# Reordering casts and weight loads at the first Strassen pair of each feed-forward block

## The chip, the cores and the metric

One core of a Trainium2 chip runs the whole kernel in one launch. The metric is the device time of that launch in microseconds, the median of several executions. The engines that matter here are TensorE (PE in the profile, with its weight loads as PEld), VectorE (DVE), ScalarE (ACT), GpSimd (POOL) and SyncE (SP); SP and POOL do nothing here but issue transfers from memory. Each engine takes its own instructions strictly in the order in which they were written out, and waits on semaphores for the others.

## The reference, cut to what matters

The computation is a two-layer decoder trunk over 512 tokens of width 1024 in float32. Each layer is a SwiGLU feed-forward block of width 2816, a mixing block (window attention, RWKV-7, short convolution), and a second feed-forward block. The change touches the feed-forward blocks alone:

```python
def swiglu(x, w_in, w_out):
    gate, up = jnp.split(x @ w_in, 2, axis=-1)
    return (jax.nn.silu(gate) * up) @ w_out

h = h + 0.5 * (1.0 + gt1) * swiglu(hn, w_ffn1_in[l], w_ffn1_out[l])
...
h = h + 0.5 * (1.0 + gt3) * swiglu(hn, w_ffn2_in[l], w_ffn2_out[l])
```

There are four such blocks: layer 0 first and second, layer 1 first and second. In the traces the first reads its weights from in_w1i, in_w1p, in_w1o and the second from in_w2i, in_w2p, in_w2o; layer 0 comes before layer 1 in time.

## The kernel before

**Precision.** Every float32 matrix is split into a high and a low part in fp32r. For weights, ScalarE casts the raw tile to `wH` (L104) and VectorE subtracts to get `wL` (L105); `hl` (L393) does both. A product then is three matmuls: high by high, high by low, low by high (L451, L452, L453 in the pairs). So each block of weights (128 x 1024, 512 KB) costs one transfer, one cast and one subtraction before its products can run, and TensorE meets first `wH` (L451) and, two matmuls later, `wL` (L453).

**A feed-forward block.** The 22 column tiles of the gate and up weights are worked off in two groups (`GROUPS`, L36): tiles 0 to 11, then 12 to 21. After each group come its products with the output weights (L93 to L95), whose results go into the residual `h` (L312). In the first group of the first block of layer 0, tiles 0 to 7 are plain products and the pairs begin at pair 4 (`n_first` is 4); in the other three blocks tiles 0 to 3 are plain and the pairs begin at pair 2 (`n_first` is 2). The second group consists of pairs 6 to 10 everywhere.

**A pair.** `pair_in(p)` (L460) computes two gate tiles and two up tiles together by Strassen's scheme with seven products instead of eight. Of the four weight blocks A(0,0), A(0,1), A(1,0), A(1,1) it makes:

- the first sum S = A(1,0) + A(1,1): SP loads the first, POOL adds the second with an accumulating transfer (`plus`, L404); product into `ps_f`, copied out by ScalarE as `up` (L470);
- the first block a11 = A(0,0), in the tile "first"; product into `ps_d`, copied out as `s1` (L474);
- the corner a12 = A(0,1), in a tile "wraw"; product into `ps_g`;
- the second sum S + a11 (VectorE, L475), product into `ps_d` on top of what is there, copied out as `s2` (L489);
- the third block A(0,0) + A(1,0), in the tile "third", again by a load and an accumulating transfer; product into `ps_d`;
- the last sum S + a12 (L502), product into `ps_f`;
- the rest, A(1,1) in a "wraw" tile, whose product (`rest`, L517) is put off and issued inside the next pair by `flush` (L386).

The tile for S alternates between "sum0" and "sum1" from pair to pair. There is one buffer each for "first", "third", "sum0" and "sum1", two for "wraw", and four for `wH` and `wL`. Between the pairs of two groups the tiles "first", "third" and "sum1" are also used for the modulation weights (`wada`, loaded by POOL, read by VectorE at L168).

**What sets the order.** A scheduler writes out the order on each engine from the dependencies and the order of the code; `tc.issue_after(x)` makes the instructions of a block that run on x's engine stand behind x. Before the change, in the first pair of a block with `n_first` 2 (`alone` is then true, L477), the cast of the second sum (`second`, L485) is held behind the copy `s1` (L474); the loads inside pairs are held behind one earlier load of the block in the first two pairs of the first group only (`after`, L565), and are otherwise free.

Of the kernel before, what the change touches and what calls it, by code (L numbers as in the profile page):

```python
# [60 lines left out]
def trunk_kernel(ctx, tc, ins, out, layers=L, phases=("ffn1", "mix", "ffn2")):  # L61
    nc = tc.nc
# [210 lines left out]
    @contextmanager  # L273
    def behind_all(marks):
        with ExitStack() as stack:
            for m in marks:
                stack.enter_context(tc.issue_after(m.ins))
            yield
# [93 lines left out]
    def ffn(l, w_in, w_pair, w_out, hn, im, ss, need, then, ready, first=None, late=None):  # L372
# [6 lines left out]
        with tc.tile_pool(name="act", bufs=1) as ap_:  # L379
# [13 lines left out]
            def hl(w):  # L393
                pair = tuple(wp.tile([P, KD, P], F32R, name=x, tag=x, bufs=4) for x in ("wH", "wL"))
                low[0] = split(*pair, w)
                return pair

            def raw(src, tag=None):
                w = (ap_.tile if tag else wp.tile)([P, KD, P], F32, name=tag or "wraw", tag=tag or "wraw", bufs=1 if tag else 2)
                with tc.issue_after(after[0].ins) if after[0] else nullcontext():  # L400
                    nc.sync.dma_start(w, src)
                return w

            def plus(w, src):  # L404
# [41 lines left out]
            def prod(pt, w, x, start, parts=(0, 1)):  # L446

                for i in parts:
                    for k in range(4):
                        wH, wL = (t[:, 4 * i + k] for t in w)  # L450
                        mm(pt[:, i], wH, x[k][0], start=start and i + k == 0, stop=False, skip_group_check=True)  # L451
                        mm(pt[:, i], wH, x[k][1], start=False, stop=False, skip_group_check=True)  # L452
                        last = mm(pt[:, i], wL, x[k][0], start=False, stop=k == 3, skip_group_check=True)  # L453
                return last
# [5 lines left out]
            def pair_in(p):  # L460
                A = lambda g, kh: w_pair[l, p, g, kh]
                turns = ("r0", "r1") if p % 2 else ("r1", "r0")
                pD, pF, pG = (psum([P, 2, H2], n, t) for n, t in zip(("ps_d", "ps_f", "ps_g"), ("mm",) + turns))
                X = new_x(p)
                half_ = lambda n: E(n).rearrange("p (i t) -> p i t", i=2)
                S = raw(A(1, 0), ("sum0", "sum1")[p % 2])
                plus(S, A(1, 1))
                prod(pF, hl(S), P1, True)
                up = half_("up")
                nc.scalar.copy(up, pF)  # L470
                a11 = raw(A(0, 0), "first")
                prod(pD, hl(a11), B11, True)
                s1 = half_("s1")
                copied = nc.scalar.copy(s1, pD)  # L474
                tt(S, S, a11, ALU.add)  # L475

                alone = p == n_first == 2  # L477
                behind = lambda m: tc.issue_after(m.ins) if p == n_first == 4 else nullcontext()
                if alone:
                    a12 = raw(A(0, 1))  # L480
                    right = hl(a12)
                    front = prod(pG, right, B21, True, (0,))
                flush()
                with tc.issue_after(copied.ins) if alone else nullcontext():
                    second = hl(S)  # L485
                with tc.issue_after(front.ins) if alone else nullcontext():
                    middle = prod(pD, second, P2, False)
                s2 = half_("s2")
                nc.scalar.copy(s2, pD)  # L489
                if alone:  # L490
                    with tc.issue_after(middle.ins):
                        back = prod(pG, right, B21, False, (1,))
                else:
                    a12 = raw(A(0, 1))
                    right = hl(a12)
                    low_ = low[0]
                    back = prod(pG, right, B21, True)
                gate = half_("gate")
                tt(gate, pG, s1, ALU.add)
                act(gate, gate, AF.Silu)  # L500
                with behind(low_) if not alone else nullcontext():
                    tt(S, S, a12, ALU.add)  # L502
                S3 = raw(A(0, 0), "third")
                plus(S3, A(1, 0))
                with behind(copied):
                    third = hl(S3)
                prod(pD, third, T3, False)
                tt(up, pD, up, ALU.add)
                with tc.issue_after(back.ins) if alone else behind(copied):
                    last = hl(S)  # L510
                    prod(pF, last, B22, False)
                tt(s2, pF, s2, ALU.add)
                act(s2, s2, AF.Silu)
                tt(up, s2, up, ALU.mult)
                put(X, hi_, up)

                def rest():  # L517
                    prod(pD, hl(raw(A(1, 1))), T4, False)
                    tt(gate, pD, gate, ALU.mult)
                    return put(X, lo_, gate)  # L520

                waiting.append(rest)
# [930 lines left out]
```

## Time and profile before

| quantity | value |
|---|---|
| median of 3 runs | 1902.75 us (1902.66 to 1906.15) |
| the profiled execution, its own time | 1905.38 us |
| its span, first to last instruction | 1903.4 us |
| TensorE busy | 1870.8 us, 98% of the span |
| VectorE busy | 1413.4 us, 74% |
| ScalarE busy | 844.8 us, 44% |
| GpSimd busy | 130.8 us, 7% |
| casts to wH at L104, one of wraw | 922 ns each, 292 of them |
| subtractions to wL at L105, one of wraw | 1059 ns each, 292 of them |
| one pair matmul at L451 | 278 ns from start to modelled end, 816 of them |
| moved by transfers | 308.46 MB, mean 162 GB/s |

Matmuls overlap: each shows some 0.28 us, but in a row without waits they start 0.11 us apart. In the timelines the columns are start in us, duration in us, engine, line and operation, output and inputs, shapes; a bracket gives how long the engine had been idle just before and what ended that. SP rows show the moment when a transfer was issued, not when its data landed. The profiled execution took 2.6 us more than the median, of which 2.0 us lie outside its span.

### The profile page before, as it was taken

To read this page: it belongs to the slowest core of one execution; us is meant where nothing else is said; L and a number is where in the kernel's file an instruction comes from. 1 tells how busy PE (TensorE), PEld (TensorE's weight loads), DVE (VectorE), ACT (ScalarE), POOL (GpSimd) and SP (SyncE) were. 2 spreads that over 40 slices of the span, in tenths; PEclk is the share of its full clock that TensorE was granted. 3 is DMA by queue.
4 is the path that set the end of the run, shared out by engine and by line. 5 is a ranking of instruction groups with operands and counts; after the bars stand their busy time and mean duration, and the time that the engine had idled before them with its cause. 6 is when DMAs were issued, how large, how long until landed. Compare 5 with 4: busy or idle time off the path is not lost. (4 is left out here: it accounts for less than half of the span.)

```text
span 1903.4 us, 37014 instructions
## 1 busy us (share of the span) xinstructions
PE 1870.8 (98%) x15460; PEld 1730.1 (91%) x15460; DVE 1413.4 (74%) x2212; ACT 844.8 (44%) x1272; POOL 130.8 (7%) x212
## 2 busy tenths in 40 slices
PE   9999999999999999999999999999999999999999
PEld 8998899887889999899899988989877999988998
DVE  7787687858876877677887776877597777864862
ACT  4453355355432554155345514544553335532551
POOL 0101101000000001100100020110000000110000
PEclk9999999999999999999999999999999999999999
DMA  7767877421221476877727687781221306774741
GB/s 301 253 174 240 254 197 238 150 70 51 69 75 54 133 199 183 279 210 199 259 74 189 170 265 228 194 269 58 92 59 48 104 24 170 205 219 132 196 140 60
DMA packets 105862, 308.46 MB, mean 162 GB/s; under 512 B 23392, under 2 KB 26464, under 8 KB 104672
## 3 DMA queue, kind: packets, MB, share of 16 engines
q1 hardware_dynamic: 77472, 203.33, 32.5%
q0 software_dynamic: 28224, 102.77, 21.4%
q8 instruction: 121, 1.98, 0.4%
q14 instruction: 45, 0.37, 0.1%
HBM read 302.66 MB, written 3.41 MB: 161 GB/s over the span
## 5 line engine op out<-in xcount | busy, mean ns | idle before, releaser
L104 ACT CAST wH<-wraw 128x1024 fp32r<-128x1024 f32 (+2 forms) x292 | 268.3, 922 | 467.5 <-PE ps_mm L94 146.2
L105 DVE TENSOR_TENSOR wL<-wraw,wH 128x1024 fp32r<-128x1024 f32 (+2 forms) x292 | 308.4, 1059 | 95.9 <-ACT wH L104 94.7
L93 PE MATMUL ps_mm<-actH,wH 128*128 128x512 f32 (+1 forms) x784 | 288.5, 368 | 0.0
L95 PE MATMUL ps_mm<-actH,wL 128*128 128x512 f32 (+1 forms) x784 | 288.1, 368 | 0.0
L94 PE MATMUL ps_mm<-actL,wH 128*128 128x512 f32 (+1 forms) x784 | 288.0, 367 | 0.0
L451 PE MATMUL ps_d<-comH,wH 128*128 128x256 f32 x816 | 226.8, 278 | 1.8 <-ACT wH L104 0.8
L453 PE MATMUL ps_d<-comH,wL 128*128 128x256 f32 x816 | 225.7, 277 | 2.3 <-DVE wL L105 2.3
L452 PE MATMUL ps_d<-comL,wH 128*128 128x256 f32 x816 | 225.4, 276 | 0.0
L168 DVE SCALAR_TENSOR_TENSOR wada<-wada,crep 128x1024 f32<-128x1024 f32 x140 | 168.0, 1221 | 59.8 <-DMA wada<-in_wadaT 59.5
L101 PE MATMUL ps_mm<-hnH,wL 128*128 128x256 f32 x976 | 199.2, 282 | 0.6 <-DVE wL L105 0.6
L101 PE MATMUL ps_mm<-hnH,wH 128*128 128x256 f32 x976 | 197.2, 282 | 0.6 <-ACT wH L104 0.3
L101 PE MATMUL ps_mm<-hnL,wH 128*128 128x256 f32 x976 | 197.0, 280 | 0.0
L105 DVE TENSOR_TENSOR wL<-sum,wH 128x1024 fp32r<-128x1024 f32 x102 | 124.9, 1224 | 71.3 <-ACT wH L104 71.1
L95 PEld LDWEIGHTS ps_mm<-actH,wL 128*128 128x128 f32 x784 | 147.8, 189 | 24.9 <-DVE wL L105 0.3
L93 PEld LDWEIGHTS ps_mm<-actH,wH 128*128 128x128 f32 x784 | 147.8, 189 | 24.2
L94 PEld LDWEIGHTS ps_mm<-actL,wH 128*128 128x128 f32 x784 | 147.8, 189 | 24.0
L104 ACT CAST wH<-sum 128x1024 fp32r<-128x1024 f32 x102 | 107.5, 1054 | 137.5 <-PE ps_d L452 59.6
L451 PEld LDWEIGHTS ps_d<-comH,wH 128*128 128x128 f32 x816 | 153.1, 188 | 4.0 <-ACT s L489 1.8
L101 PEld LDWEIGHTS ps_mm<-hnH,wL 128*128 128x128 f32 x976 | 149.5, 188 | 7.9 <-issue 6.6
L101 PEld LDWEIGHTS ps_mm<-hnH,wH 128*128 128x128 f32 x976 | 148.6, 188 | 8.4 <-issue 5.1
L453 PEld LDWEIGHTS ps_d<-comH,wL 128*128 128x128 f32 x816 | 153.2, 188 | 2.9 <-DVE wL L105 2.9
L101 PEld LDWEIGHTS ps_mm<-hnL,wH 128*128 128x128 f32 x976 | 149.3, 188 | 5.2 <-issue 4.9
(432 smaller groups left out, 4312.2 us busy)
## 6 DMA issues: line engine op xcount, KB each, us to landing
wada<-in_wadaT POOLq DMA_DIRECT2D x128, 512.0 KB, 5.2
wraw<-in_wmi SPq DMA_DIRECT2D x40, 512.0 KB
wraw<-in_w2p SPq DMA_DIRECT2D x36, 512.0 KB
wraw<-in_w1p SPq DMA_DIRECT2D x32, 512.0 KB
wraw<-in_w1o SPq DMA_DIRECT2D x32, 384.0 KB
wraw<-in_w2o SPq DMA_DIRECT2D x32, 384.0 KB
wraw<-in_w1i SPq DMA_DIRECT2D x20, 512.0 KB
wraw<-in_w1o SPq DMA_DIRECT2D x32, 320.0 KB
```

The costliest lines, as they stand in the source:

```text
L93: mm(acc, wH, xH, start=start, stop=False)
L94: mm(acc, wH, xL, start=False, stop=False)
L95: mm(acc, wL, xH, start=False, stop=stop)
L101: mm(acc[:, sl], w[a][:, k], x[b][:, sl], start=start and n == 0 and sl is HALVES[0], stop=stop and n == 2, skip_group_check=True)
L104: nc.scalar.copy(hi, src)
L105: return nc.vector.tensor_sub(lo, src, hi.bitcast(F32))
L168: stt(w, w, 1.0, crep, ALU.mult, ALU.mult, accum_out=out_)
L451: mm(pt[:, i], wH, x[k][0], start=start and i + k == 0, stop=False, skip_group_check=True)
L452: mm(pt[:, i], wH, x[k][1], start=False, stop=False, skip_group_check=True)
L453: last = mm(pt[:, i], wL, x[k][0], start=False, stop=k == 3, skip_group_check=True)
```

## The change

The change does three things, in `raw` and `pair_in`:

1. In the first pair of a block with `n_first` 2, the cast of the second sum is held behind the copy of the first sum's product (`taken`, the copy to `up`) instead of behind the copy `s1`; the cast of the third block takes its place behind `s1`; and in the pair after it the cast of the first sum is held behind the copy `s2`.
2. Loads of pairs get an order on SP: the third block's load behind the corner's, and a pair's first-sum load behind the first block's load of the pair before it. This holds in all pairs of a block.
3. Every load is recorded in `order` under its name. Loads without a name are recorded under None, and loads without `after_` look up None: so the loads of first block, corner and rest are held behind the unnamed load that was traced last (a first sum, third block or rest).

```diff
-            def raw(src, tag=None):
+            order = {}
+
+            def raw(src, tag=None, name=None, after_=None):
                 w = (ap_.tile if tag else wp.tile)([P, KD, P], F32, name=tag or "wraw", tag=tag or "wraw", bufs=1 if tag else 2)
-                with tc.issue_after(after[0].ins) if after[0] else nullcontext():
-                    nc.sync.dma_start(w, src)
+                with behind_all([m for m in (after[0], order.get(after_)) if m]):
+                    order[name] = nc.sync.dma_start(w, src)
                 return w
...
-                S = raw(A(1, 0), ("sum0", "sum1")[p % 2])
+                S = raw(A(1, 0), ("sum0", "sum1")[p % 2], after_="a11")
                 plus(S, A(1, 1))
-                prod(pF, hl(S), P1, True)
+                with behind_all([order["s2"]] if p == n_first + 1 == 3 else ()):
+                    S_ = hl(S)
+                prod(pF, S_, P1, True)
                 up = half_("up")
-                nc.scalar.copy(up, pF)
-                a11 = raw(A(0, 0), "first")
+                taken = nc.scalar.copy(up, pF)
+                a11 = raw(A(0, 0), "first", "a11")
...
-                    a12 = raw(A(0, 1))
+                    a12 = raw(A(0, 1), None, "a12")
...
-                with tc.issue_after(copied.ins) if alone else nullcontext():
+                with tc.issue_after(taken.ins) if alone else nullcontext():
                     second = hl(S)
...
-                nc.scalar.copy(s2, pD)
+                order["s2"] = nc.scalar.copy(s2, pD)
...
-                    a12 = raw(A(0, 1))
+                    a12 = raw(A(0, 1), None, "a12")
...
-                S3 = raw(A(0, 0), "third")
+                S3 = raw(A(0, 0), "third", after_="a12")
                 plus(S3, A(1, 0))
-                with behind(copied):
+                with tc.issue_after(copied.ins) if alone else behind(copied):
                     third = hl(S3)
```

The order of TensorE's instructions is the same before and after. What moves on the other engines is shown at three places (of the numbers in the names, those on the tiles of one pair tell the pairs apart; after the change the lines stand 2 to 4 further down).

**ScalarE, first pair (pair 2) of the second block of layer 0**, from the copy `up` to the copy `s2`; sum_7832 is the pair's sum tile, cast as first, second and last sum in turn. Before:

```order
L470 COPY up<-ps_f 128x512
L474 COPY s_7895<-ps_d 128x512
L104 CAST wH<-sum_7832 128x1024
L104 CAST wH<-third 128x1024
L104 CAST wH<-sum_7832 128x1024
L489 COPY s_7944<-ps_d 128x512
```

With the change:

```order
L474 COPY up<-ps_f 128x512
L104 CAST wH<-sum_7832 128x1024
L478 COPY s_7895<-ps_d 128x512
L104 CAST wH<-third 128x1024
L104 CAST wH<-sum_7832 128x1024
L493 COPY s_7944<-ps_d 128x512
```

The second sum's cast now stands ahead of the copy `s1` (s_7895); nothing else of these six moved. Both blocks of layer 1 that begin this way, and this one, change alike.

**SP, first pair of the second group (pair 6) of the first block of layer 1**: wraw_13030 is its corner, third_13064 its third block, first_12967 its first block, wraw_13200 its rest; sum1_13134 is the first sum of pair 7. Before:

```order
L401 DMA wraw_13030<-in_w1p 128x1024
L401 DMA third_13064<-in_w1p 128x1024
L401 DMA sum1_13134<-in_w1p 128x1024
L401 DMA first_12967<-in_w1p 128x1024
L401 DMA wraw_13200<-in_w1p 128x1024
```

With the change:

```order
L403 DMA wraw_13030<-in_w1p 128x1024
L403 DMA third_13064<-in_w1p 128x1024
L403 DMA first_12967<-in_w1p 128x1024
L403 DMA sum1_13134<-in_w1p 128x1024
L403 DMA wraw_13200<-in_w1p 128x1024
```

The first block's load now stands ahead of the next pair's sum. The second block of layer 0 changes in the same way at its pair 6, and in both VectorE's sum S + a11 now stands ahead of the residual of output tile 6 instead of behind it.

**SP, first two pairs (4 and 5) of the first block of layer 0**: wraw_1513 is the corner of pair 4, wraw_1683 its rest, first_1450 its first block; sum1_1617 and first_1650 belong to pair 5. Before:

```order
L401 DMA wraw_1513<-in_w1p 128x1024
L401 DMA wraw_1683<-in_w1p 128x1024
L401 DMA third_1547<-in_w1p 128x1024
L401 DMA first_1450<-in_w1p 128x1024
L401 DMA sum1_1617<-in_w1p 128x1024
L401 DMA first_1650<-in_w1p 128x1024
```

With the change:

```order
L403 DMA wraw_1513<-in_w1p 128x1024
L403 DMA third_1547<-in_w1p 128x1024
L403 DMA first_1450<-in_w1p 128x1024
L403 DMA sum1_1617<-in_w1p 128x1024
L403 DMA wraw_1683<-in_w1p 128x1024
L403 DMA first_1650<-in_w1p 128x1024
```

The rest of pair 4 moved from the second place to behind the first sum of pair 5.

## The prediction

> **What bounds the kernel now.** I read the page first, then TensorE's waits over the whole span, then the timelines of the engines around those waits that lie in the pairs.
>
> ```profile
> span 1903.4 us, 37014 instructions
> PE 1870.8 (98%) x15460; PEld 1730.1 (91%) x15460; DVE 1413.4 (74%) x2212; ACT 844.8 (44%) x1272; POOL 130.8 (7%) x212
> ```
>
> TensorE sets the time. Its order doesn't change, so the change can only move its waits. TensorE's list of waits (total, times, longest, in us) has two rows that come up in several blocks of pairs:
>
> ```profile
> PE ps_d L453 <- DVE wL L105: 3.5, 5, 0.8
> PE ps_d L451 <- ACT wH L104: 1.8, 4, 1.0
> ```
>
> The timeline places them: of the five and four, three each are the second sum of the first pair in the three blocks with `n_first` 2, all three alike; one each is a first block in layer 1; the last is layer 0's first block. Here is one of the three, in the second block of layer 0:
>
> ```profile
> 674.80 0.28 PE L453 MATMUL ps_g<-hnH,wL 128*128 128x256 f32 x1
> 675.34 0.39 PE L451 MATMUL ps_d<-comH,wH 128*128 128x256 f32 x1 [0.26 <-ACT wH L104]
> ...
> 676.60 0.38 PE L453 MATMUL ps_d<-comH,wL 128*128 128x256 f32 x1 [0.76 <-DVE wL L105]
> 676.82 0.28 PE L451 MATMUL ps_d<-comH,wH 128*128 128x256 f32 x1
> 676.93 0.28 PE L452 MATMUL ps_d<-comL,wH 128*128 128x256 f32 x1
> ```
>
> Undisturbed matmuls start 0.113 us apart, as here from 676.82 to 676.93 (the rows are rounded). From 674.80 to 676.82 there are four steps, which need 0.45 us and took 2.02. So the place costs **1.57 us**, more than the 1.02 of the brackets, since each wait also empties TensorE's pipeline.
>
> **Part A, the second sum ahead of `s1`: gain 4.7.** Why it was late, on ScalarE and VectorE:
>
> ```profile
> 670.99 0.58 ACT L470 COPY up<-ps_f 128x512 f32<-128x512 f32 x1 [0.69 <-PE ps_f L453]
> 673.75 0.59 ACT L474 COPY s<-ps_d 128x512 f32<-128x512 f32 x1 [2.17 <-PE ps_d L453]
> 674.24 1.05 ACT L104 CAST wH<-sum 128x1024 fp32r<-128x1024 f32 x1
> ```
> ```profile
> 666.69 1.22 DVE L475 TENSOR_TENSOR sum<-sum,first 128x1024 f32<-128x1024 f32 x1
> ...
> 675.32 1.23 DVE L105 TENSOR_TENSOR wL<-sum,wH 128x1024 fp32r<-128x1024 f32 x1 [4.29 <-ACT wH L104]
> ```
>
> The sum itself is ready at 667.91. ScalarE stands idle for 2.17 us in front of `s1`, with the cast queued behind it. With the change the cast runs at 671.6 to 672.6 inside that idle time, and `wL`, on a VectorE that is idle for 4.29 us, until 673.9. TensorE asks for them at 674.91 and 675.14: both waits go, with 1.2 us in hand. `s1` is not delayed, as TensorE releases it only at 673.75. The third block's cast stands behind `s1` as before; VectorE now adds the corner before it subtracts for the third block, which is then done near 676.5, while TensorE, after 24 products of the second sum and 12 of the corner, asks at 674.91 + 36 x 0.113 = 679.0. Nothing late takes the place. Three blocks: 3 x 1.57 = 4.7. Bounds: 4.7, and 2.0 if a shorter wait remains at each.
>
> The same edit moves the third block's load behind the corner's, some ten microseconds later on SP; its cover is that its cast isn't wanted before 674.3 (priced under the rivals).
>
> **Part B and C, the first block ahead of the next pair's sum.** At the head of the second group the buffers of all three loads come free late, and they queue. Layer 1, first block (SP, POOL, then VectorE):
>
> ```profile
> 1149.01 0.33 SPq L401 DMA_DIRECT2D sum<-in_w1p  x1
> 1150.44 0.33 SPq L401 DMA_DIRECT2D first<-in_w1p  x1
> ```
> ```profile
> 1150.97 0.88 POOL L405 DMA_DIRECT2D third<-in_w1p  x1 [12.09 <-DVE mod L192]
> ```
> ```profile
> 1158.23 1.23 DVE L475 TENSOR_TENSOR sum<-sum,first 128x1024 f32<-128x1024 f32 x1 [4.93 <-DMA first<-in_w1p]
> ...
> 1163.04 0.74 DVE L312 SCALAR_TENSOR_TENSOR h<-ps_mm,cg,h 128x512 f32<-128x512 f32 x1
> 1163.70 1.22 DVE L105 TENSOR_TENSOR wL<-wraw,wH 128x1024 fp32r<-128x1024 f32 x1
> ```
>
> The first block needs 7.8 us from issue to landing (1150.44 to 1158.23), behind a sum that pair 7 wants only later. From its landing VectorE needs 6.69 us until the corner's `wL` is done (1158.23 to 1164.92). What TensorE makes of it:
>
> ```profile
> 1158.00 0.28 PE L453 MATMUL ps_f<-comH,wL 128*128 128x256 f32 x1
> 1159.33 0.39 PE L451 MATMUL ps_d<-hnH,wH 128*128 128x256 f32 x1 [1.05 <-ACT wH L104]
> ...
> 1160.64 0.39 PE L453 MATMUL ps_d<-hnH,wL 128*128 128x256 f32 x1 [0.81 <-DVE wL L105]
> ...
> 1164.87 0.28 PE L451 MATMUL ps_g<-hnH,wH 128*128 128x256 f32 x1
> ```
> ```profile
> 1161.30:1164.70 3.40, 3.40 (x18) 3.40 (x17) 3.37 (x4) 1.69 (x3) 0.00 (x0) 0.50 0.57 164
> ```
>
> From 1158.00 to the corner's start at 1164.87 lie 25 steps, 2.83 us at full rate: 4.04 us are lost, and only about half is in the brackets. In the row of stretches the granted clock is 0.50 for the 3.4 us behind the waits, which costs 1.7. But that part is not free to win on its own: at full clock TensorE would have been at the corner by 1163.2 and waited for its `wL` until 1164.92 all the same. The landing of the first block sets this place.
>
> [...]
>
> With the change the first block goes out at 1150.44 with no sum ahead. A lone 512 KB load takes 3.9 us: the sum issued at 117.17 has landed when POOL goes on at 121.09 (rows under D). So it lands near 1154.3; other end, no earlier than before. VectorE's chain gets one residual more in its way (0.74 at most in its row, of which a wait for ScalarE hides a little; I take 0.5): corner ready at 1154.3 + 6.7 + 0.5 = 1161.5, where TensorE wants it at 1161.07. So a **new wait** of about 0.5 appears there. Next late is `s1`: on ScalarE the cast of the third block stands ahead of it, for which the accumulating transfer of 1150.97 has to land, 8.9 us later:
>
> ```profile
> third<-in_w1p POOLq DMA_DIRECT2D x1, 512.0 KB, 8.9
> ```
>
> That is 1159.9, plus cast 1.05, `up` 0.58, last cast 1.05 and `s1` 0.58: 1163.1. TensorE's second sum, which started 38 steps behind 1158.00 (4.3 us needed, so 1162.3 at best), starts near 1163.2. Its row before:
>
> ```profile
> 1166.59 0.38 PE L451 MATMUL ps_d<-comH,wH 128*128 128x256 f32 x1
> ```
>
> Gain **C = 3.3**; bounds 1.0 (it lands halfway) and 4.2 (nothing left but the steps).
>
> Layer 0, second block, **B**, is the same with less at stake:
>
> ```profile
> 818.67 0.39 PE L453 MATMUL ps_g<-hnH,wL 128*128 128x256 f32 x1 [1.04 <-DVE wL L105]
> ```
> ```profile
> 805.78 0.33 SPq L401 DMA_DIRECT2D first<-in_w2p  x1
> ```
> ```profile
> 811.91 1.23 DVE L475 TENSOR_TENSOR sum<-sum,first 128x1024 f32<-128x1024 f32 x1 [3.42 <-DMA first<-in_w2p]
> ```
>
> Landing 811.91, with the change 805.78 + 3.9 = 809.7, so 2.2 earlier. The loss is 1.04 and 0.27 of refilling, 1.3; minus the residual's 0.5 there is 1.7 of room to cover it. The `s1` copy comes next here too, so I take **B = 1.1**, bounds 0.3 and 1.3.
>
> **Part D, a loss in layer 0's first block.**
>
> ```profile
> 129.16 0.39 PE L451 MATMUL ps_d<-comH,wH 128*128 128x256 f32 x1 [0.47 <-ACT s L489]
> ```
> ```profile
> 97.99 2.49 SPq L401 DMA_DIRECT2D wraw<-in_w1p  x2
> ...
> 117.17 0.33 SPq L401 DMA_DIRECT2D sum<-in_w1p  x1
> ```
> ```profile
> 121.09 0.86 POOL L405 DMA_DIRECT2D sum<-in_w1p  x1 [12.35 <-DMA sum<-in_w1p]
> ```
> ```profile
> 127.57 1.05 ACT L104 CAST wH<-sum 128x1024 fp32r<-128x1024 f32 x1 [1.66 <-DMA sum<-in_w1p]
> ```
>
> TensorE's third block waits for the copy `s2`, which stands on ScalarE behind the cast of pair 5's first sum, which waits for the accumulating transfer issued at 121.09. The rest of pair 4, loaded at about 100 in the double row of 97.99, now goes out right behind the sum, at 117.5, and its 512 KB pass while the accumulation runs. The accumulation took 6.4 us with one load beside it; the next one in that block, less crowded, took 5.2:
>
> ```profile
> sum<-in_w1p POOLq DMA_DIRECT2D x1, 512.0 KB, 6.4
> ...
> third<-in_w1p POOLq DMA_DIRECT2D x1, 512.0 KB, 5.2
> ```
>
> So a load beside it costs up to 1.2; this one has partly passed by then. **D = -0.7**, bounds 0 and a whole load's 2.3. It goes to TensorE in full.
>
> [...]
>
> In the second group of layer 1's second block SP's order moves too, but there the casts come from 6 to 12 us after the loads and TensorE has no wait; I cost it at nothing, and if that cover went it would cost about what B gains.
>
> **Sum.** 4.7 + 1.1 + 3.3 - 0.7 = 8.4 off the profiled span of 1903.4: 1895.0. The median of the runs, 1902.75, lies 2.6 below the profiled execution's own 1905.38; I take the same 8.4 off it: **1894.4**.
>
> **Rivals.**
>
> *New waits take the place in B and C.* The landing gains only part, as three loads and two accumulations still share the engines; for it speaks the first block's 7.8 us against 3.9, of which the sum may not be the whole cause. Then B 0.3, C 1.0, D -1.0: 4.7 + 0.3 + 1.0 - 1.0 = 5.0, **1897.8**.
>
> *Transfers take A back.* In the output products behind each first group ScalarE waits for loads; if these don't come earlier, A is lost there and B + C + D = 3.7 remain: **1899.1**. Against it: TensorE has no such wait in its list, and the loads start when buffers come free, which moves forward with TensorE.
>
> *Slower: the third block comes too late.* Its accumulation starts some ten microseconds later and now meets the other loads of the first pair, and its cast stands ahead of the last cast and of `s2`. It decides from a landing of about 676.6 on, from where each microsecond costs one in each of three blocks. Estimated from the rows: 657.2 + 3.9 + 8.9 = 670.0. To be slower it has to land past 681; at 682, 3 x 5.4 - 8.4 = 7.8 lost, **1910.5**.
>
> *It doesn't do what it says:* a further dependency keeps the second cast where it was. Its place on ScalarE is ahead of `s1`, and the sum is done 3.7 us before; then **1899**.
>
> **Numbers.** Forecast 0.62, new waits 0.20, transfers 0.10, doesn't do it 0.03, slower 0.05. 0.2% is about what a measurement of this kernel can tell from no change, 3.8 us, so faster means below 1898.95: the forecast whole (0.62) and most of the first rival (0.14), 0.76; same: the rest of these, 0.19; slower 0.05. The best case of all bounds is 4.7 + 1.3 + 4.2 - 0 = 10.2, 1892.5; the worst of the forecast's own 4.7 + 0.3 + 1.0 - 2.3 = 3.7, 1899. The range is **1892.0 to 1899.4**.
>
> **What would show it.** A: no bracket on the second sum's L451 and L453 in three blocks. C: first block landing near 1154, full clock behind it, a small wait at the corner or the second sum. B: L453 of the corner without its bracket. D: the wait on L489 in layer 0's first block grown from 0.47 to 1.2. I am wrong if brackets come up at the third block or at L93 to L95, or if first blocks still take over 6 us to land.

## The result and the profile after

The changed kernel takes 1897.7 us (median of 12 runs, 1895.15 to 1901.98), the kernel before 1903.77 on the same chip (12 runs): ratio **0.997, 95% interval 0.9962 to 0.9978**, faster by 4 to 7 us. In a second set of runs the ratio was 0.9966 (0.9953 to 0.998). The forecast was 1894.4, with a range of 1892.0 to 1899.4: the sign and the range hold, the time is 3.3 us above the forecast. Of that, 1.0 us is the kernel before itself, whose median of 1902.75 in three runs became 1903.77 in twelve; the other 2.3 us are gain that did not come, and the experiments show why. The profiled execution took 1895.63, 9.75 less than the one of before, which is more than the medians differ: the one of before lay 1.6 us above its median of twelve runs, the one of the changed kernel 2.1 us below its own.

The page of the changed kernel, its span and the busy times of the engines:

```profile
span 1893.6 us, 37004 instructions
PE 1865.6 (99%) x15460; PEld 1726.1 (91%) x15460; DVE 1414.5 (75%) x2212; ACT 845.6 (45%) x1272; POOL 130.7 (7%) x212
```

TensorE's waits after the change, the rows of the pairs and their surroundings (total, times, longest, in us):

```profile
PE ps_d L453 <- ACT s L493: 0.9, 1, 0.9
...
PE ps_ss L231 <- DVE ss L340: 0.6, 1, 0.6
PE ps_d L455 <- DVE wL L105: 0.6, 1, 0.6
PE ps_mm L95 <- DVE wL L105: 0.6, 1, 0.6
```

Of the five waits on the second products and four on the first ones that stood under `ps_d` (lines 453 and 451 of before, 455 and 453 now), one is left, in layer 0's first block. New are two waits in the close of that block (L95, L231); the second profile of this kernel doesn't have them.

**A**, second block of layer 0, the place that the prediction quotes:

```profile
671.61 0.59 ACT L474 COPY up<-ps_f 128x512 f32<-128x512 f32 x1 [1.38 <-PE ps_f L455]
672.09 1.06 ACT L104 CAST wH<-sum 128x1024 fp32r<-128x1024 f32 x1
673.18 1.23 DVE L105 TENSOR_TENSOR wL<-sum,wH 128x1024 fp32r<-128x1024 f32 x1 [2.23 <-ACT wH L104]
674.37 0.59 ACT L478 COPY s<-ps_d 128x512 f32<-128x512 f32 x1 [1.22 <-PE ps_d L455]
```
```profile
675.42 0.28 PE L455 MATMUL ps_g<-hnH,wL 128*128 128x256 f32 x1
675.53 0.28 PE L453 MATMUL ps_d<-comH,wH 128*128 128x256 f32 x1
675.64 0.28 PE L454 MATMUL ps_d<-comL,wH 128*128 128x256 f32 x1
675.76 0.28 PE L455 MATMUL ps_d<-comH,wL 128*128 128x256 f32 x1
```

The cast runs right behind `up`, `wL` is done by 674.4, and TensorE goes from the corner into the second sum at its step of 0.11 with no bracket. The copy `s1` still waits for TensorE (1.22), so nothing was put off.

**C**, layer 1's first block of pair 6, and the stretch in which before had its half-rate clock:

```profile
1145.68 0.33 SPq L403 DMA_DIRECT2D first<-in_w1p  x1
1146.06 0.42 SPq L403 DMA_DIRECT2D sum<-in_w1p  x1
...
1149.56 1.23 DVE L479 TENSOR_TENSOR sum<-sum,first 128x1024 f32<-128x1024 f32 x1 [1.68 <-DMA first<-in_w1p]
...
1153.75 0.28 PE L455 MATMUL ps_f<-comH,wL 128*128 128x256 f32 x1
1153.87 0.28 PE L453 MATMUL ps_d<-hnH,wH 128*128 128x256 f32 x1
...
1155.55 1.22 DVE L105 TENSOR_TENSOR wL<-wraw,wH 128x1024 fp32r<-128x1024 f32 x1
...
1156.64 0.28 PE L453 MATMUL ps_g<-hnH,wH 128*128 128x256 f32 x1
```
```profile
1151.30:1154.70 3.40, 3.40 (x32) 3.40 (x31) 3.37 (x4) 1.60 (x2) 0.87 (x1) 1.00 1.06 237
```

The first block goes out ahead of the sum and lands 3.9 us after its issue; 7.2 us later the corner's `wL` is done (1156.77), as TensorE asks for it. The clock stays at 1.00.

**B** and **D**: in layer 0's second block the same load lands 3.7 us after its issue, and the corner's bracket of 1.04 is gone; the wait for `s2` in layer 0's first block is 0.94, where it was 0.47.

```profile
803.91 0.33 SPq L403 DMA_DIRECT2D first<-in_w2p  x1
```
```profile
807.62 1.23 DVE L479 TENSOR_TENSOR sum<-sum,first 128x1024 f32<-128x1024 f32 x1 [1.66 <-DMA first<-in_w2p]
```
```profile
128.86 0.39 PE L453 MATMUL ps_d<-comH,wH 128*128 128x256 f32 x1 [0.94 <-ACT s L493]
```

Laid matmul by matmul over the profile before, TensorE gains 4.74 at the three second sums (1.57, 1.59, 1.58), 0.95 at B, 3.75 at C and 1.07 in the start-up, and loses 0.77 at D and 1.14 at the two new waits; the rest of the 9.8 us is in pieces below 0.4. So far everything seems to have gone as forecast. But this is one execution of each kernel.

### The profile page after: what moved, and what is told of

Its sections match the earlier page's. It is cut to its first block, busy times and chain, and to the rows that moved or that the text cites. A ratio compares the mean times of both kernels' runs of the same rounds, so it can differ in the third digit from the quotient of the medians.

```text
span 1893.6 us, 37004 instructions
## 1 busy us (share of the span) xinstructions
PE 1865.6 (99%) x15460; PEld 1726.1 (91%) x15460; DVE 1414.5 (75%) x2212; ACT 845.6 (45%) x1272; POOL 130.7 (7%) x212
## 3 DMA queue, kind: packets, MB, share of 16 engines
HBM read 302.66 MB, written 3.41 MB: 162 GB/s over the span
## 5 line engine op out<-in xcount | busy, mean ns | idle before, releaser
L95 PE MATMUL ps_mm<-actH,wL 128*128 128x512 f32 (+1 forms) x784 | 288.1, 368 | 0.6 <-DVE wL L105 0.6
L455 PE MATMUL ps_d<-comH,wL 128*128 128x256 f32 x816 | 225.3, 276 | 0.0
L95 PEld LDWEIGHTS ps_mm<-actH,wL 128*128 128x128 f32 x784 | 147.8, 189 | 25.3 <-DVE wL L105 1.0
L454 PEld LDWEIGHTS ps_d<-comL,wH 128*128 128x128 f32 x816 | 153.2, 188 | 0.0
```

What stands on the lines that cost most here:

```text
L95: mm(acc, wL, xH, start=False, stop=stop)
```

## Experiments

Two theories stood against each other. The prediction's: each term is a property of the order of instructions, and the profile before shows its size. The rival: only A is; the waits that hang on a load differ from one execution to the next, and the profile before showed a bad one.

**1. The two halves of the change apart.** One kernel keeps ScalarE's order alone:

```diff
-                with behind_all([m for m in (after[0], order.get(after_)) if m]):
+                with behind_all([m for m in (after[0],) if m]):
```

> The changed kernel without the order of loads on SP: only ScalarE's and VectorE's order of the first pair is kept (second sum's cast behind `taken`, third block's cast behind `s1`, pair 3's first sum's cast behind `s2`). My theory: part A is won whole and nothing else, 3 x 1.57 = 4.7 us of span, ratio 0.9975; the three pairs of brackets on the second sum (L451 and L453 of before) are gone, the first block of layer 1's pair 6 still takes about 7.8 us from issue to landing with its two waits (1.05 and 0.81) and a 3.4 us stretch at clock 0.50 behind them, the corner's wait of 1.04 in layer 0's pair 6 stays, and the wait for `s2` in layer 0's first block stays at 0.47. Rival (A needs the loads' order as well, since the third block's accumulation ahead of the corner's load is what makes room): less than 2 us, ratio 0.999 or more, with new brackets on the third block or the corner in the first pairs. Rival (all of the gain is one half-rate stretch of TensorE's clock): the time is that of before.

The other keeps SP's order alone:

```diff
-                with behind_all([order["s2"]] if p == n_first + 1 == 3 else ()):
-                    S_ = hl(S)
+                S_ = hl(S)
-                with tc.issue_after(taken.ins) if alone else nullcontext():
+                with tc.issue_after(copied.ins) if alone else nullcontext():
-                with tc.issue_after(copied.ins) if alone else behind(copied):
+                with behind(copied):
                     third = hl(S3)
```

> The kernel before with only the order of loads on SP (corner and first block ahead of third block and next sum). My theory: B + C - D = 1.1 + 3.3 - 0.7 = 3.7 by the prediction, 1.0 + 3.75 - 0.77 = 4.0 by the changed kernel's trace, ratio 0.998; the three second sums keep their brackets (about 0.26 to 0.3 and 0.76 each, 1.57 lost at each), the first block of layer 1's pair 6 lands 3.8 to 4 us after its issue, no stretch at clock 0.50 in the pairs, and the wait for `s2` in layer 0's first block is about 0.9. Rival (the two orders help each other): less than 2 us, ratio over 0.999. Rival (the loads' order alone hurts, as the third block's accumulation comes later while its cast still stands ahead of `s1`... of the second sum): slower than before by some microseconds, with brackets on the third block in the first pairs.

Measured: ScalarE's order alone 1900.01, ratio 0.9971 (0.9956 to 0.9986); SP's alone 1903.4, ratio 0.9999 (0.9985 to 1.0014). The first is nearly the whole gain, the second nothing that can be measured, where 3.7 to 4.0 were expected. In the profile of SP's order alone A's brackets stand as before, three pairs of them (the fourth wait on L455 is in layer 0's first block):

```profile
PE ps_d L455 <- DVE wL L105: 3.0, 4, 0.8
...
PE ps_d L453 <- ACT wH L104: 0.8, 3, 0.3
```

The surprise is in the profile of ScalarE's order alone, which has SP's old order in the second group: B and C were missing there too. In layer 1 the first block went out behind the sum at 1144.78 and had landed by 1150.12, 5.3 us later instead of 7.8, and TensorE did not wait. No theory so far had a way for ScalarE's order to do that. So neither expectation was right about C, and more profiles were needed.

**2. The same kernels again.**

> The kernel before, unchanged, for a second profile of it. The question: are the losses that the prediction called B and C there in every execution? In the profile that the prediction reads, layer 1's first block of pair 6 landed 7.8 us after its issue; with ScalarE's order alone changed and the same order on SP it took 5.3 us (issue 1144.78, residual's add at 1150.12) and TensorE did not wait there. Theory now: B and C differ between executions with the speed of the transfers and with how far the adaLN weights lag TensorE; this profile then shows the three second sums with 1.57 us lost each, as before, but another C (0 to 4). Rival (the prediction): C is the order's own, so 1.05 and 0.81 of brackets come up again within 0.3, with a landing 7 to 8 us after the issue; then ScalarE's order would have removed it by some way not seen.

> The kernel before, a third profile, for the same question and the same numbers: brackets of 1.57 us in all at each of the three second sums in any case; C and B between 0 and 4, and 0 and 1.3, if they belong to the execution; 4.0 and 1.3 once more if they belong to the order of the loads.

> ScalarE's order alone, a second profile. If C belongs to the execution, this kernel, whose order on SP in the second group is that of before, may show it in a second profile though the first had none: a landing of the first block more than 6 us after its issue goes with brackets at its L453 and L455, one under 5.5 with none. If ScalarE's order had removed C, no bracket is there again, whatever the landing. A is gone in either case.

> The changed kernel once more, for another profile of it. In its first profile the places outside the parts A to D are not level with before: 0.67 us lost at 345 to 352 (a wait of L95 for VectorE's L105) and 0.47 at 366 to 370 (a wait of L231 for VectorE's L340), both in the close of layer 0's first block, and 1.07 gained by 55 us, where a half-rate stretch of the clock stands at another place of the start-up. Theory: these are differences between executions, not the change: this profile has them at other sizes (some below 0.2), while A's brackets stay away and C's first block lands within 4 us of its issue. Rival: the change moved transfers there (SP's order differs up to the second group), and both waits come back within 0.1 us at the same instructions. The time: ratio 0.997 to before, and of two executions the one with the higher granted clock is the faster.

A came up at the same size in both further profiles of before (brackets of 0.26 and 0.75 to 0.76 at all three sums). C did not. The second profile of before, its SP and VectorE rows in the timeline:

```profile
1148.13 0.33 SPq L401 DMA_DIRECT2D first<-in_w1p  x1
...
1153.06 1.23 DVE L475 TENSOR_TENSOR sum<-sum,first 128x1024 f32<-128x1024 f32 x1 [2.07 <-DMA first<-in_w1p]
```

4.9 us, and no wait behind it: this execution took 1899.7. The third took 1905.19, with a landing after 6.7 us and 1.4 us lost. The second profile of ScalarE's order alone had C worse than any before it:

```profile
1146.13 0.33 SPq L403 DMA_DIRECT2D first<-in_w1p  x1
...
1154.91 1.23 DVE L479 TENSOR_TENSOR sum<-sum,first 128x1024 f32<-128x1024 f32 x1 [5.92 <-DMA first<-in_w1p]
...
1156.01 0.39 PE L453 MATMUL ps_d<-hnH,wH 128*128 128x256 f32 x1 [1.90 <-ACT wH L104]
...
1157.33 0.39 PE L455 MATMUL ps_d<-hnH,wL 128*128 128x256 f32 x1 [0.81 <-DVE wL L105]
```

The rival holds: how large C is belongs to the execution. The second profile of the changed kernel (median 1897.35, ratio 0.9966) had neither wait of the close of layer 0's first block, so these 1.14 us were that execution's as well, as was the 1.07 of the start-up.

**3. Which of the two rules for loads acts.** Without the sum behind the first block, and without the third block behind the corner:

```diff
-                S = raw(A(1, 0), ("sum0", "sum1")[p % 2], after_="a11")
+                S = raw(A(1, 0), ("sum0", "sum1")[p % 2])
```

> The changed kernel without one of the two rules for loads: the next pair's sum no longer waits behind the first block, so it goes out ahead of it again, as before; the corner still goes ahead of the third block. In ten profiles the first block of pair 6 landed 3.6 to 4.0 us after its issue wherever this rule was there (layer 0's second block and layer 1's first), and 4.9 to 8.8 us where it was not. Theory: this rule alone does that, so here it lands 4.9 us or more after its issue at both places, with a loss at layer 1's first block between 0 and 4.6 by execution (what the landing comes later than 3.3 us before TensorE's last product of the sum); A stays whole. Time between that of ScalarE's order alone and that of the changed kernel, 1898 to 1900.5, ratio 0.997 to 0.998. Rival (the corner's place ahead of the third block's does it): 3.6 to 4.0 again and the time of the changed kernel, 1897.5.

```diff
-                S3 = raw(A(0, 0), "third", after_="a12")
+                S3 = raw(A(0, 0), "third")
```

> The changed kernel without the other rule: the third block's load goes out ahead of the corner's again in the first pairs, as before; the first block stays ahead of the next pair's sum. Theory: the time of the changed kernel, 1897.5, ratio 0.997; the first block of pair 6 lands 3.6 to 4.0 us after its issue at both places, and no bracket comes up in the first pairs, whose third block and corner had time in every profile. Rival (the corner's load has to come first for A): brackets at the corner of the first pairs, 1 us or more at each, 1900 or more.

Without the first rule the landing took 8.4 us and the waits were there; without the second it took 3.9 and no bracket came up in the first pairs. The times, 1898.35 and 1897.95, both ratio 0.9966 (0.9953 to 0.9979 and 0.9954 to 0.9978), don't tell them apart; the profiles, one of each kernel, do. No rule for the third block was needed for the landing.

```profile
1145.41 0.33 SPq L403 DMA_DIRECT2D first<-in_w1p  x1
...
1153.76 1.23 DVE L479 TENSOR_TENSOR sum<-sum,first 128x1024 f32<-128x1024 f32 x1 [5.50 <-DMA first<-in_w1p]
...
1154.87 0.39 PE L453 MATMUL ps_d<-hnH,wH 128*128 128x256 f32 x1 [0.57 <-ACT wH L104]
...
1156.18 0.39 PE L455 MATMUL ps_d<-hnH,wL 128*128 128x256 f32 x1 [0.81 <-DVE wL L105]
...
1160.51 0.39 PE L455 MATMUL ps_g<-hnH,wL 128*128 128x256 f32 x1 [1.25 <-DVE wL L105]
```

**4. Does the landing set the place?** The first block of pair 6 loaded twice (`twice` is set for `a11` where `p` is 6):

```diff
                     order[name] = nc.sync.dma_start(w, src)
+                    if twice:
+                        order[name] = nc.sync.dma_start(w, src)
```

> The changed kernel with the first block of pair 6 loaded twice into the same buffer, in each of the four blocks (the second load waits for the first, so it lands later by one whole load; what stands behind it on SP goes out later too). Theory (C's mechanism): the landing sets when the corner's weights are cast. In the changed kernel's profile layer 1's first block landed at 1149.56, 3.9 after its issue; 3.9 later and 7.2 us on to the corner's weights is 1160.7, where TensorE wants them at about 1156.4: it loses about 4 us in layer 1's first block, some 2 to 4 in layer 0's two, and nothing to 1 in layer 1's second block, whose casts come 6 us and more after the loads; 8 to 12 us in all. Rival (another transfer set the place and the first block has slack): under 1 us at each place, 3 in all.

```profile
1148.07 0.33 SPq L403 DMA_DIRECT2D first<-in_w1p  x1
...
1151.76 0.33 SPq L405 DMA_DIRECT2D first<-in_w1p  x1
...
1157.60 1.23 DVE L481 TENSOR_TENSOR sum<-sum,first 128x1024 f32<-128x1024 f32 x1 [6.68 <-DMA first<-in_w1p]
...
1158.70 0.39 PE L455 MATMUL ps_d<-hnH,wH 128*128 128x256 f32 x1 [1.33 <-ACT wH L104]
```

One execution, 1903.09. TensorE lost 4.0 in layer 1's first block, 3.8 in layer 0's second, nothing in layer 1's second, as the theory said, and nothing in layer 0's first, where it had said 2 to 4: there the block still landed 5.7 us ahead of TensorE. So 7.8 in all, just under the 8 to 12. The landing sets the place, but the landing itself was not as forecast: in layer 1 the second load, at the head of SP's queue, took 5.8 us (1151.76 to 1157.60) and not 3.9. That the loss came out at the forecast 4 is in part luck, as this execution had 1 us more between the first issue and TensorE's last product of the sum than the first profile of the changed kernel.

Over all profiles, layer 1, pair 6 (from the timelines; "ahead" is from the landing to the start of the first sum's last product on TensorE; "lost" is the time of the next 85 matmuls less 85 x 0.1134 and less the 0.78 us that remain where nothing disturbs them; "GpSimd" is what the DMA view shows its queue to have moved between issue and landing, in MB):

| order of the loads | profile | issue to landing | GpSimd | ahead | lost |
|---|---|---|---|---|---|
| sum first | before, 1st / 2nd / 3rd | 7.8 / 4.9 / 6.7 | 0.45 / 0.01 / 0.25 | -0.2 / 3.4 / 2.1 | 4.0 / 0.0 / 1.4 |
| sum first | ScalarE alone, 1st / 2nd / 3rd | 5.3 / 8.8 / 8.0 | 0.03 / 0.61 / 0.45 | 4.1 / -1.1 / -0.1 | 0.0 / 4.6 / 3.8 |
| sum first | no rule for the sum | 8.4 | 0.57 | 0.3 | 3.1 |
| block first | changed, 1st / 2nd | 3.9 / 3.7 | 0 / 0 | 4.2 / 4.2 | 0.2 / 0.1 |
| block first | SP alone; no rule for the third | 3.8; 3.9 | 0; 0 | 4.4; 5.1 | 0.1; 0.0 |
| block first | the two kernels of experiment 5 | 3.7; 3.7 | 0; 0 | 3.8; 5.0 | 1.0; 0.1 |
| block first, twice | experiment 4, from the first issue | 9.5 | 0.41 (second load) | -0.5 | 4.0 |

Three things can be read off. The order separates the landings: 3.7 to 3.9 us with the block first and loaded once, 4.9 to 8.8 behind the sum. Behind the sum the landing is the later the more GpSimd's accumulating loads have moved by then; with the block first it comes before they move anything. And the loss follows the landing one for one once it comes later than about 3.4 us ahead (-0.2 ahead: 3.6 by that rule, 4.0 measured; -1.1: 4.5 and 4.6; 0.3: 3.1 and 3.1). The mean loss is 2.4 behind the sum and 0.3 without it, so C is worth **2.2 on the average** (over seven and six profiles, an interval of some 1.8 on either side), between 0 and 4.6 in one execution. At B the same count gives 0.2 (0 to 1.0) and 0.1.

**5. The wait of part D.** In one kernel pair 5's first sum is cast behind `s2` in layer 0's first block too; in another the loads' order is asked for only where a name is given as well, so that the rest of pair 4 loads early again.

```diff
-                with behind_all([order["s2"]] if p == n_first + 1 == 3 else ()):
+                with behind_all([order["s2"]] if p == n_first + 1 else ()):
```

> The changed kernel with pair 5's first sum cast behind `s2` in layer 0's first block too, and nothing else. Theory: the wait of TensorE's third block for `s2` (0.52 to 0.97 in the three profiles with the change's order, 0.35 to 1.17 without it) is gone, and 0.8 to 1.2 of TensorE's time with it; the time is 1896.5, ratio 0.9962, if nothing new comes. Rival (it comes back later): in the profile of the kernel with both edits a wait of 0.80 for `s1` stood in pair 6 of that block at 236.01, which no other profile has; if that belongs to the cast's place, it is here too at about 230 to 236 with 0.5 to 1.0, and the time is that of the changed kernel, 1897.5. If it is absent here, it belonged to that execution.

```diff
-                with behind_all([m for m in (after[0], order.get(after_)) if m]):
+                with behind_all([m for m in (after[0], order.get(after_) if after_ else None) if m]):
-                with behind_all([order["s2"]] if p == n_first + 1 == 3 else ()):
+                with behind_all([order["s2"]] if p == n_first + 1 else ()):
```

> The changed kernel with two things put right in what part D names: the load order is recorded and asked for only where a name is given, so that the rest of pair 4 loads early again, as before; and in layer 0's first block too pair 5's first sum is cast behind `s2`. My theory: the wait of TensorE's third block for `s2` (0.94 in the changed kernel's trace, 0.47 before) is gone; as pair 5's first sum comes only after the third block, the cast has some 2.7 us left, which is enough unless its accumulation lands later than 127; so about 1.0 to 1.2 us better than the changed kernel, ratio to before 0.9963. Rival (the cast behind `s2` is late for pair 5's first product, or the early load meets another transfer): no better than the changed kernel, 0.997 or more, with a bracket on pair 5's first sum or on layer 0's second group.

The wait for `s2` is gone in both, worth 0.8 at the place when the first is laid over the second profile of the changed kernel. In the times it can't be found: 1898.91, ratio 0.9968 (0.9955 to 0.998), and 1897.27, ratio 0.9961 (0.9947 to 0.9975); the means of their 20 runs and of the 23 of the changed kernel differ by 0.2 with an interval of 1.4 on either side. The wait of 0.80 in pair 6 of layer 0's first block did not come up in the first of them, while the third profile of ScalarE's order alone, with the old place of the cast, has 1.07 there: it belongs to executions too. What did come up, in the first, is the `s1` copy in layer 1, the next one late that the prediction named:

```profile
1161.54 0.39 PE L453 MATMUL ps_d<-comH,wH 128*128 128x256 f32 x1 [0.61 <-ACT s L478]
```

**6. What the loads' order is worth in the times.**

> ScalarE's order alone, timed once more and with a third profile, so that the worth of the loads' order can be told from two sets of runs. Theory: the first block of layer 1's pair 6 lands 4.9 to 8.8 us after its issue, and TensorE loses there what the landing comes later than 3.3 us before its last product of the sum (0 to 4.6). The mean of five such profiles is 2.0 at that place and 0.2 at layer 0's, so the mean time lies some 2 us above the changed kernel's 1897.9: 1899.5 to 1900.5, ratio 0.9975 to 0.998. Rival (the loads' order is worth nothing, as its own two-kernel comparison with before says): 1898 or less.

1898.37, ratio 0.9969 (0.9958 to 0.998), between what the theory and the rival said, with a landing after 8.0 us and 3.8 lost. The 20 runs of ScalarE's order alone have a mean of 1899.2, the 23 of the changed kernel 1897.9: 1.4 apart, with 1.5 on either side. SP's order alone against before: 0.1 apart, with 1.7 on either side. The two comparisons together, weighted, put the loads' order at 0.8 us with 1.1 on either side. The profiles make it 2.2 with 1.8 on either side; the two agree only within their intervals, and the times don't settle whether it is worth anything.

## Why the prediction was right, and where it was not

- **A, 4.7: right to 0.1.** 4.74 in the profile, the same at each of the three sums in every profile with the old order, gone in every one with the new. The whole chain held: the idle ScalarE, `wL` by 674.4 (forecast 673.9, in an execution whose `up` came 0.6 later), `s1` not put off, the third block in time. Timed alone it gives 5.2 in the mean, with 1.4 on either side.
- **B, 1.1 and C, 3.3: right mechanism, wrong size.** The landing came 3.9 after the issue, as the lone load said, and the corner was ready 7.2 us behind it, which is the forecast 6.7 + 0.5 to the tenth. The step that failed is the one before: that the 7.8 us from issue to landing, and with it the loss of 4.04, was what the order costs. It was one draw from 4.9 to 8.8. C is 2.2 and B 0.1 on the average. The 0.9 that the forecast kept back at C for a late `s1` was needed in one of six profiles with the block first (1.0 lost, most of it at 1161.54), elsewhere 0.2 or less.
- **D, -0.7: not shown.** The wait grew from 0.47 to 0.94 between the two profiles, but it is 0.35 to 1.17 in six profiles with the early load (mean 0.77) and 0.51 to 1.48 in six without (mean 0.89). A tenth of a microsecond is what is left. The accumulation that was to take up to 1.2 us longer took 6.4 to 6.9 us in the six (mean 6.7) and 6.4 to 7.3 in the others (mean 6.8). No run shows the 2.3 that bounds the term: it is at most an estimate, what 512 KB take at the 229 GB/s that all queues together moved from 121.09 to 127.57 in the profile before. What the runs showed in its place is the 0.1 between these two means.
- **The same 8.4 off the median: the failed step's second half.** With the means in place, 4.74 + 2.2 + 0.1 - 0.1 = 6.9; the means of 23 runs and of 61 of before differ by 6.6, with 1.1 on either side. The profile of before showed more loss than its median run has, and the median can't gain what it doesn't lose. That this execution lay 2.6 above the median was in the prediction, but only as an offset, and the account of it ahead of the prediction, 2.0 us outside the span, is wrong: every execution has some 2.0 there (1895.63 against 1893.6 in the changed kernel). The 2.6 lie inside the span, where this execution lost 4.0 at C and 1.0 at B.
- **The clock.** The forecast that the half-rate stretch is not free to win fits what was measured. With it, the places that landed -0.2, -0.1 and -1.1 us ahead lost 0.1 to 0.4 more than the landing's rule gives; without it (loaded twice, and no rule for the sum) 0.1 and 0.0. A later wait for the corner, 1.25 in the rows above, takes its place.
- **The rivals.** No wait for the third block's weights came up, and the change did what it says. In the output products, where the prediction named any wait as a sign of being wrong, one of 0.6 came up in the first profile of the changed kernel (L95, close of layer 0's first block) and in none of the others. New waits in place of the old (1897.8) is the nearest in time, for another reason: nothing new took the gain, there was less to gain.

## What to carry to other kernels

A wait that comes up at the same size in every repetition of a place (1.57, 1.59 and 1.58 us at the three second sums) is the order's own, and its price can be read from one profile to a tenth of a microsecond. A wait on a load that stands once in a profile (C: 0 to 4.6 us by execution) is one draw: take a second profile, or price it from zero to what the row shows, before subtracting it from a median. Where a load shares its queue with one that is wanted later, issue the one wanted first ahead of it (here it landed after 3.7 to 3.9 us instead of 4.9 to 8.8), though the mean gain may be too small to be timed.

## What the runs showed of the hardware

**Half the clock behind stretches half full of work.** In the profile before the granted clock is 0.50 from 17.86 to 21.27, from 1161.32 to 1164.74 and in the last 1.4 us; in the profile after from 13.18 to 16.59 alone. Each but the last is 3.41 us long, and the first two of the profile before begin 1143.46 us apart, 335 times 3.4133. The first ones of the two profiles begin 4.68 us apart, no multiple of that: the phase differs between these executions. In the start-up half rate came behind stretches in which TensorE was busy for 3.21 and 3.36 us; at C, and at the other places listed below, it came behind stretches in which TensorE was busy for 1.55 to 2.00 us of 3.41, even where the idle time came in two pieces. Two rows each, the stretch with the waits and the next (PE busy is the second number, the granted clock stands third from the end), for layer 1's C place in the second profile of ScalarE's order alone and in the kernel without the rule for the sum:

```profile
1155.11:1158.52 3.41, 1.70 (x12) 1.50 (x13) 3.36 (x3) 3.13 (x4) 0.00 (x0) 1.00 0.72 142
1158.52:1161.93 3.41, 3.41 (x18) 3.30 (x17) 3.38 (x5) 1.80 (x3) 0.00 (x0) 0.50 0.37 136
```
```profile
1154.23:1157.65 3.42, 2.04 (x15) 1.77 (x15) 3.33 (x4) 3.14 (x4) 0.00 (x0) 1.00 0.77 155
1157.65:1161.06 3.41, 2.16 (x18) 1.97 (x18) 3.41 (x4) 2.40 (x4) 0.00 (x0) 1.00 0.34 135
```

Half rate followed the 1.70, in two pieces of idle time (the waits of 1.90 and 0.81 quoted in experiment 2), and not the 2.04. It also followed 1.55 in the profile before (1157.91 to 1161.32), 1.73 in experiment 4 (811.31 to 814.73), 1.88 in the first kernel of experiment 5 (rows below) and 2.00 in the second profile of the changed kernel (528.78 to 532.20); it did not follow 1.82 in experiment 4 (1156.06 to 1159.48) or 1.99 in the profile after (rows below). So these rows overlap between 1.82 and 2.00 and give no sharp limit.

**The same waits, another price.** In the mixing block at 526 to 532 every profile has the same two waits, 1.00 and 1.42 (within 0.01, but 1.04 in three for the first). Where in a stretch of 3.41 us they fall is a matter of phase: the wait of 1.42 ends 2.62 us into the first of these stretches in the profile after and 1.48 into it in the first kernel of experiment 5:

```profile
528.59:532.00 3.41, 1.99 (x12) 1.24 (x13) 3.25 (x8) 0.70 (x2) 0.00 (x0) 1.00 0.02 5
532.00:535.42 3.42, 2.91 (x53) 1.88 (x51) 1.26 (x5) 0.00 (x0) 0.00 (x0) 1.00 0.00 0
```
```profile
529.06:532.47 3.41, 1.88 (x24) 1.37 (x23) 2.42 (x6) 0.70 (x2) 0.00 (x0) 1.00 0.00 0
532.47:535.88 3.41, 3.35 (x38) 2.07 (x38) 1.48 (x5) 0.00 (x0) 0.00 (x0) 0.50 0.00 0
```

In the second, half rate holds for two stretches (the 28 matmuls of L1022 at 536.09 take 1.71 us, where they take 0.98 in the profile after), and from the end of the wait to L1041 it takes 10.97 us instead of 8.63. Laid over the first profile of before, half rate costs 2.2 to 2.4 us in the four profiles that have it; one of them is the second profile of the changed kernel. A second such place is at 1460: 11.00 us between the same two instructions in the first kernel of experiment 5, 8.65 in the profile before. Of the changed kernel's first 12 runs the six with a granted clock of 0.998 or 0.999 have a median of 1896.4, the six below it 1898.8.

**The load's landing went with what else the queues carried.** With the block first, in the profile after, the sum went out 0.38 us behind it and an accumulating load 0.52 behind it, and it still took 3.9; the accumulation moved nothing before that landing. Behind a sum issued 1.4 us earlier it took 4.9 to 8.8. In those seven profiles SP's queue moved 1.3 to 1.5 MB between issue and landing, GpSimd's queue 0.01 MB at 4.9 us and 0.61 at 8.8, at 236 to 261 GB/s in all (1.43 MB, 0.45 MB and 242 GB/s in the first profile of before); a later landing also leaves more time for this, so the numbers alone don't tell cause from effect. But place in the queue was not everything: the second load of experiment 4 stood at the head of SP's queue while the accumulation was already moving, 0.41 MB of it, and took 5.8. Why the accumulation caught the first block in some executions and not in others, no run shows.
